# A Winograd-style 3x3 convolution: all input pairs as fp32 through one queue into nine fixed homes

## The chip, the cores and the metric

The kernel runs on one core of one Trainium2 chip. The metric is the device time in microseconds (us) of one execution; lower is better. Beside it stands a profile of one execution, whose span is the time from its first to its last instruction.

## The reference

A 3x3 convolution with padding 1, stride 1, over 16 images of 64 channels and 64 x 64 points, to 128 output channels, all in fp32:

```python
batch, c_in, h, w, c_out = 16, 64, 64, 64, 128
x_pad = np.pad(x, ((0, 0), (0, 0), (1, 1), (1, 1)), mode='constant')
for b in range(batch):
    for co in range(c_out):
        for ci in range(c_in):
            for kh in range(3):
                for kw in range(3):
                    output[b, co] += weight[co, ci, kh, kw] * x_pad[b, ci, kh:kh+h, kw:kw+w]
```

The input has 16.8 MB, the output 33.6 MB, the weights 0.3 MB.

## The kernel before

Two images make a pair: their 2 x 64 channels fill the 128 partitions, so a pair is one tile of 128 x 64 x 64 (16 KB per partition in fp32, 2 MB in all). There are eight pairs, p = 0 to 7.

Output rows are made two at a time. For rows 2j and 2j+1 the kernel makes three sums of products on TensorE: one over x[2j] + x[2j+1] with the middle weight row (group U), one for the even rows (group A, weight rows G21 and G0) and one for the odd rows (group Bt, G01 and G2). The output is A + U and Bt + U. The pair sums x[2j] + x[2j+1] are the tile `ss`, made by `sums` (line 76) on GpSimd, for pair 0 on VectorE. The fp16 input itself is the tile `xs`. A pair is cut into four blocks of 16 output rows. In each block TensorE runs U, A, Bt (line 150) into PSUM (8 banks, two for each group), ScalarE copies U to SBUF as `ut` (line 164), and VectorE adds it to A and Bt into the fp32 output tiles `ots` (lines 174 and 177), one tile for each of the two images.

Input comes in two ways. Pairs 0 to 3 are loaded in fp32 on SyncE's queue at the start (lines 45 and 49), as `x0` and `xf`, and ScalarE casts them to `xs` (line 101 for pair 0; line 169 for the others, four casts of 16 rows, two each in blocks 2 and 3 of the pair before). Pairs 4 to 7 are loaded by GpSimd's queue, and the transfer itself casts to fp16 (`load`, line 67): pair 4 before pair 0's work, pairs 5, 6, 7 after the sums issued in pairs 1, 2, 3.

Output goes out by `store` (line 106): the first image of a pair on SyncE's queue when its last block is added, the second image held back and issued on ScalarE's queue behind the first U copies of the next block (line 171). The last pair goes out in halves of 32 rows.

The tiles `x0`, `xf` and `ot` share one pool of eight places of 16 KB per partition (`opool`), taken in turn: pairs 0 to 3 take four places as input, the outputs of pairs 0 and 1 the other four, those of pairs 2 and 3 the input's places, those of pair 4 the places of pair 0's outputs, and so on. A place is written again only when its load's readers or its store are done. `xs` has five places of 8 KB, `ss` three, `ut` four. `keep` pins an instruction behind what was written before it on its own engine; the stores on SyncE and the loads on lines 42 to 49 are not pinned.

Of the kernel before, what the change touches and what calls it, by code (L numbers as in the profile page):

```python
# [8 lines left out]
F32 = mybir.dt.float32  # L9
F16 = mybir.dt.float16  # L10


@with_exitstack
def kernel(
    ctx: ExitStack,
    tc: tile.TileContext,
    x: bass.AP,
    weight: bass.AP,
    out: bass.AP,
):  # L20
    nc = tc.nc
    B, CI, H, W = x.shape
    CO = weight.shape[0]
    assert H == 64 and W == 64 and CI == 64 and CO == 128 and B % 2 == 0
    NP = B // 2
    RB = 8

    keep = tc.keep_in_program_order
    x_rows = x.rearrange("b c h w -> (b c) h w")
    out_rows = out.rearrange("b co h w -> b co h w")  # L30
    w_flat = weight.rearrange("co ci kh kw -> co (ci kh kw)")

    const = ctx.enter_context(tc.tile_pool(name="const", bufs=1))
    psum = ctx.enter_context(tc.tile_pool(name="psum", bufs=8, space=bass.MemoryType.PSUM))
    xpool = ctx.enter_context(tc.tile_pool(name="xpool", bufs=5))
    opool = ctx.enter_context(tc.tile_pool(name="opool", bufs=8))
    spool = ctx.enter_context(tc.tile_pool(name="spool", bufs=3))
    upool = ctx.enter_context(tc.tile_pool(name="upool", bufs=4))


    w_raw = const.tile([CO, CI * 9], F32)
    nc.sync.dma_start(w_raw, w_flat)
    x0 = opool.tile([128, H, W], F32, tag="ot", name="x0")
    cuts = [(0, 18), (18, 34), (34, 50), (50, 64)]
    nc.sync.dma_start(x0, x_rows[0:128, :, :])
    xf = {}
    for p in (1, 2, 3):
        xf[p] = opool.tile([128, H, W], F32, tag="ot", name="xf")
        nc.sync.dma_start(xf[p], x_rows[128 * p : 128 * p + 128, :, :])
    zeros = const.tile([128, 512], F16)  # L50
    keep(nc.vector.memset(zeros, 0.0))  # L51
    warm = psum.tile([128, 512], F32, tag="acc", name="warm")

    def spin(n):
        for _ in range(n):
            keep(nc.tensor.matmul(warm, zeros[:, 0:128], zeros))  # L56

    ident = const.tile([128, 128], F16)
    make_identity(nc, ident)
    w16 = const.tile([CO, CI * 9], F16)  # L60
    keep(nc.gpsimd.tensor_copy(w16, w_raw))  # L61

    xs = {p: xpool.tile([128, H, W], F16, tag="xs", name="xs") for p in range(4)}

    def load(p):
        xs[p] = xpool.tile([128, H, W], F16, tag="xs", name="xs")
        keep(nc.gpsimd.dma_start(xs[p], x_rows[128 * p : 128 * p + 128, :, :]))  # L67

    ss = {}

    def sums(eng, p, src, lo, n):
        if p not in ss:
            ss[p] = spool.tile([128, H // 2, W], F16, tag="ss", name="ss")
        v = src.rearrange("p (j i) c -> p j i c", i=2)
        keep(
            eng.tensor_add(  # L76
                ss[p][:, lo : lo + n, :], v[:, lo : lo + n, 0, :], v[:, lo : lo + n, 1, :]
            )
        )


    Wt = const.tile([128, 5, 3, CO], F16)
    G0, G21, G1, G01, G2 = range(5)

    def wrow(i):
        return Wt[:, i, :, :].rearrange("p t c -> p (t c)")

    for kh, g in ((1, G1), (2, G2), (0, G0)):
        wp = psum.tile([128, 512], F32, tag="acc", name="wp")
        for k in range(3):  # L90
            t = 3 * kh + k
            for q in (0, 64):
                keep(nc.tensor.matmul(wp[q : q + 64, k * CO : k * CO + CO], w16[:, t::9], ident))  # L93
        keep(nc.scalar.copy(wrow(g), wp[:, 0 : 3 * CO]))  # L94
    spin(10)
    keep(nc.gpsimd.tensor_sub(wrow(G21), wrow(G2), wrow(G1)))  # L96
    keep(nc.gpsimd.tensor_sub(wrow(G01), wrow(G0), wrow(G1)))  # L97
    load(4)
    for n, (lo, hi) in enumerate(cuts):
        sums(nc.vector, 0, x0, RB * n, RB)  # L100
        keep(nc.scalar.copy(xs[0][:, lo:hi, :], x0[:, lo:hi, :]))  # L101

    held = []

    def store(eng, p, b2, ot, lo, hi):
        return eng.dma_start(
            out_rows[2 * p + b2, :, lo:hi, :],
            ot.rearrange("p j i c -> p (j i) c")[:, lo:hi, :],
        )

    for p in range(NP):
        if p + 1 < NP:
            for lo in (0, 16):
                sums(nc.gpsimd, p + 1, xf.get(p + 1, xs[p + 1]), lo, 16)
        if p > 0 and p + 4 < NP:
            load(p + 4)
        ots = [
            opool.tile([128, H // 2, 2, W], F32, tag="ot", name="ot") for _ in range(2)
        ]
        for blk in range(4):  # L120
            j0 = blk * RB

            def group(wi_rows):

                tiles = [
                    psum.tile([128, RB, W], F32, tag="acc", name="acc") for _ in range(2)
                ]
                n = 3 * len(wi_rows)
                i = 0
                for wi, off in wi_rows:  # L130
                    for kw in (1, 0, 2):
                        c_lo, c_hi = max(0, 1 - kw), min(W, W + 1 - kw)
                        for b2 in range(2):
                            p0 = 64 * b2
                            lo, hi = j0, j0 + RB
                            if off is None:
                                rhs = ss[p][p0 : p0 + 64, lo:hi, c_lo + kw - 1 : c_hi + kw - 1]
                            else:
                                while 2 * lo + off < 0:
                                    lo += 1  # L140
                                while 2 * (hi - 1) + off > H - 1:
                                    hi -= 1
                                first = 2 * lo + off
                                last = 2 * (hi - 1) + off
                                rhs = xs[p][
                                    p0 : p0 + 64,
                                    first : last + 1 : 2,
                                    c_lo + kw - 1 : c_hi + kw - 1,
                                ]
                            nc.tensor.matmul(  # L150
                                tiles[b2][:, lo - j0 : hi - j0, c_lo:c_hi],
                                Wt[p0 : p0 + 64, wi, kw, :],
                                rhs,
                                start=i == 0,
                                stop=i == n - 1,
                            )
                        i += 1
                return tiles

            U = group([(G1, None)])  # L160
            us = []
            for b2 in range(2):
                ut = upool.tile([128, RB, W], F32, tag="ut", name="ut")
                keep(nc.scalar.copy(ut, U[b2]))  # L164
                us.append(ut)
            if p + 1 in xf:
                q = p + 1
                for lo in {2: (0, 16), 3: (32, 48)}.get(blk, ()):
                    keep(nc.scalar.copy(xs[q][:, lo : lo + 16, :], xf[q][:, lo : lo + 16, :]))  # L169
            while held:  # L170
                keep(store(nc.scalar, *held.pop(0)))
            A = group([(G21, 1), (G0, -1)])
            for b2 in range(2):
                nc.vector.tensor_add(ots[b2][:, j0 : j0 + RB, 0, :], A[b2], us[b2])  # L174
            Bt = group([(G01, 0), (G2, 2)])
            for b2 in range(2):
                nc.vector.tensor_add(ots[b2][:, j0 : j0 + RB, 1, :], Bt[b2], us[b2])  # L177
            parts = {3: (0, 64)} if p < NP - 1 else {1: (0, 32), 3: (32, 64)}
            if blk in parts:
                lo, hi = parts[blk]  # L180
                store(nc.sync, p, 0, ots[0], lo, hi)
                held.append((p, 1, ots[1], lo, hi))
    while held:
        keep(store(nc.scalar, *held.pop(0)))


# [28 lines left out]
```

## Time and profile before

| | |
|---|---|
| time, median of 3 runs (lowest to highest) | 126.33 us (126.21 to 126.34) |
| the profiled execution | 126.56 us |
| its span | 124.8 us |
| mean granted TensorE clock | 0.963 |
| first product of pair 0 (line 150) | 9.92 us |
| time from pair to pair (ScalarE's stores) | 12.81 us |

Times in a view are microseconds from the start of the span, unless marked ns. PE is TensorE (matmul), PEld its weight loads, DVE VectorE, ACT ScalarE, POOL GpSimd, SP SyncE; SPq, ACTq and POOLq are their instruction queues. A row with forty digits cuts the span into forty slices of 3.12 us and gives the busy share of each in tenths (9 is 90% or more); the DMA row is the mean over the core's 16 DMA engines, and the GB/s row is what they moved, where a casting transfer is counted by the bytes that it writes. A DMA queue's line has packets, MB, and the time that its packets took as a share of the time of 16 engines. A line of instructions has start, length, engine, source line, operation, output <- input, count, and in brackets the idle time before it and what ended that. A line of DMA issues has the count, KB of one transfer and the median time from issue to landing.

### The profile page before, as it was taken

How to read it: one execution, taken by the hardware profiler on the slowest of the kernel's cores; microseconds unless marked ns; L12 is line 12 of the kernel's file. 1: busy time of each engine (PE TensorE's matmuls, PEld its weight loads, DVE VectorE, ACT ScalarE, POOL GpSimd, SP SyncE). 2: the span in 40 equal slices, each digit the busy share in tenths (PEclk: the TensorE clock that was granted, in tenths of full speed). 3: DMA queues.
4: the chain of work that ended last, by engine and by line, in shares of the span. 5: the costliest groups of instructions: out<-in, count | busy, mean ns of one | idle time of the engine just before them, and what ended most of it. 6: DMA issues, size and time to landing. Idle time of an engine off the chain costs nothing.

```text
span 124.8 us, 2437 instructions
## 1 busy us (share of the span) xinstructions
PE 108.2 (87%) x988; PEld 49.3 (40%) x988; DVE 82.8 (66%) x133; ACT 52.0 (42%) x84; POOL 36.2 (29%) x27
## 2 busy tenths in 40 slices
PE   0699999999999999999999999999999999990000
PEld 0433444444444444444444444444444444440000
DVE  0016787878878787877777778777877787685000
ACT  4319749833993399333333333333333333330000
POOL 2360086294799202920067000940000000000000
PEclk9999999999999999999999999999999999999555
DMA  6899999999999999999999999999999999999991
GB/s 173 362 436 407 297 323 349 425 315 415 397 349 368 305 376 373 360 334 362 381 347 360 334 344 412 431 431 425 425 441 420 436 415 425 436 412 418 436 402 74
DMA packets 3898, 46.57 MB, mean 373 GB/s; under 512 B 432, under 2 KB 432, under 8 KB 560
## 3 DMA queue, kind: packets, MB, share of 16 engines
q1 hardware_dynamic: 2016, 25.46, 49.5%
q10 hardware_dynamic: 1296, 16.78, 31.6%
q0 software_dynamic: 576, 4.19, 16.1%
q8 instruction: 7, 0.11, 0.3%
q14 instruction: 3, 0.02, 0.0%
HBM read 17.07 MB, written 33.55 MB: 406 GB/s over the span
## 4 chain that ended last, share of the span: by engine, by line
PE 86%; DMA 2%; DVE 1%; issue 1%; POOL 1%; DVEq 0%
PE acc L150 81%; PE warm L56 4%; DMA w_raw<-in_weight_dram 2%; PE wp L93 1%; DVE ot L174 1%; POOL w L61 1%; DVE ot L177 0%; DVEq L210 0%; DVEq L174 0%
## 5 line engine op out<-in xcount | busy, mean ns | idle before, releaser
L150 PE MATMUL acc<-xs,Wt 64*128 64x504 f16 (+3 forms) x768 | 87.0, 373 | 0.0
L150 PEld LDWEIGHTS <-Wt 64*128 64x128 f16 x960 | 46.8, 94 | 56.2 <-issue 0.8
L164 ACT COPY ut<-acc 128x512 f32<-128x512 f32 x64 | 34.3, 588 | 52.9 <-issue 32.1
L174 DVE TENSOR_TENSOR ot<-acc,ut 128x512 f32<-128x512 f32 x64 | 41.2, 686 | 22.6 <-PE acc L150 18.3
L177 DVE TENSOR_TENSOR ot<-acc,ut 128x512 f32<-128x512 f32 x64 | 41.1, 684 | 0.0
L150 PE MATMUL acc<-ss,Wt 64*128 64x504 f16 (+1 forms) x192 | 26.0, 377 | 0.0
L76 POOL TENSOR_TENSOR ss<-xs 128x1024 f16<-128x1024 f16 x8 | 16.8, 2124 | 20.2 <-DMA xs<-in_x_dram 20.2
L76 POOL TENSOR_TENSOR ss<-xf 128x1024 f16<-128x1024 f32 x6 | 14.1, 2361 | 13.6 <-DMA xf<-in_x_dram 13.6
L169 ACT CAST xs<-xf 128x1024 f16<-128x1024 f32 x12 | 12.0, 1058 | 0.0
L76 DVE TENSOR_TENSOR ss<-x 128x512 f16<-128x512 f32 x4 | 2.5, 687 | 7.7 <-DMA x<-in_x_dram 7.7
L93 PE MATMUL wp<-ident,w 128*64 128x128 f16 x18 | 1.3, 328 | 4.3 <-POOL w L61 4.3
L101 ACT CAST xs<-x 128x1024 f16<-128x1024 f32 (+2 forms) x4 | 3.9, 1042 | 2.6 <-DMA x<-in_x_dram 2.6
L67 POOL DMA_DIRECT2D xs<-in_x_dram x4 | 2.4, 600 | 7.8 <-ACT xs L169 7.8
L56 PE MATMUL warm<-zeros 128*128 128x512 f16 x10 | 4.4, 631 | 0.0
L93 PEld LDWEIGHTS <-w 128*64 128x64 f16 x18 | 1.1, 210 | 4.3 <-POOL w L61 4.3
L94 ACT CAST Wt<-wp 128x384 f16<-128x384 f32 x3 | 1.2, 487 | 2.9 <-PE wp L93 2.9
L56 PEld LDWEIGHTS <-zeros 128*128 128x128 f16 x10 | 1.3, 143 | 2.3 <-issue 2.2
L94 ACT ACT_TABLE_LOAD x1 | 1.3, 1283 | 0.7 <-PEq L199 0.7
L96 POOL TENSOR_TENSOR Wt<-Wt 128x384 f16<-128x384 f16 x1 | 0.9, 907 | 1.7 <-ACT Wt L94 1.7
L61 POOL CAST w<-w_raw 128x576 f16<-128x576 f32 x1 | 0.7, 663 | 2.3 <-DMA w_raw<-in_weight_dram 2.3
L97 POOL TENSOR_TENSOR Wt<-Wt 128x384 f16<-128x384 f16 x1 | 0.9, 910 | 0.0
L51 DVE MEMSET zeros<- 128x256 uint32 x1 | 0.3, 272 | 0.9 <-PEq L199 0.9
(6 smaller groups left out, 0.9 us busy)
## 6 DMA issues: line engine op xcount, KB each, us to landing
out_dram<-ot SPq DMA_DIRECT2D x7, 2048.0 KB, 22.0
out_dram<-ot ACTq DMA_DIRECT2D x7, 2048.0 KB, 18.9
xf<-in_x_dram SPq DMA_DIRECT2D x3, 2048.0 KB, 22.1
xs<-in_x_dram POOLq DMA_DIRECT2D x4, 1024.0 KB, 23.4
x<-in_x_dram SPq DMA_DIRECT2D x1, 2048.0 KB, 7.6
out_dram<-ot SPq DMA_DIRECT2D x2, 1024.0 KB, 10.6
out_dram<-ot ACTq DMA_DIRECT2D x2, 1024.0 KB, 11.0
w_raw<-in_weight_dram SPq DMA_DIRECT2D x1, 288.0 KB, 2.8
```

What stands on the lines that cost most here:

```text
L56: keep(nc.tensor.matmul(warm, zeros[:, 0:128], zeros))
L61: keep(nc.gpsimd.tensor_copy(w16, w_raw))
L67: keep(nc.gpsimd.dma_start(xs[p], x_rows[128 * p : 128 * p + 128, :, :]))
L76: eng.tensor_add(ss[p][:, lo : lo + n, :], v[:, lo : lo + n, 0, :], v[:, lo : lo + n, 1, :])
L93: keep(nc.tensor.matmul(wp[q : q + 64, k * CO : k * CO + CO], w16[:, t::9], ident))
L94: keep(nc.scalar.copy(wrow(g), wp[:, 0 : 3 * CO]))
L101: keep(nc.scalar.copy(xs[0][:, lo:hi, :], x0[:, lo:hi, :]))
L150: nc.tensor.matmul(tiles[b2][:, lo - j0 : hi - j0, c_lo:c_hi], Wt[p0 : p0 + 64, wi, kw, :], rhs, start=i == 0, stop=i == n - 1,)
L164: keep(nc.scalar.copy(ut, U[b2]))
L169: keep(nc.scalar.copy(xs[q][:, lo : lo + 16, :], xf[q][:, lo : lo + 16, :]))
L174: nc.vector.tensor_add(ots[b2][:, j0 : j0 + RB, 0, :], A[b2], us[b2])
L177: nc.vector.tensor_add(ots[b2][:, j0 : j0 + RB, 1, :], Bt[b2], us[b2])
```

## The change

All eight pairs are loaded in fp32 on SyncE's queue, and ScalarE casts all of them (seven pairs on line 169's place). No load casts and GpSimd issues no DMA. The pool of eight places becomes nine homes with names, each of 16 KB per partition: E has two, T three, a, b, c and d one each.

- E first holds pairs 0 and 1 (one transfer each), then pairs 5 and 6 (one transfer, issued on SyncE behind pair 1's store), then the outputs of pair 7.
- T first holds pairs 2, 3 and 4 (one transfer of 6 MB, issued at the start behind pairs 0 and 1), then pair 7 in its first third (issued behind pair 3's store) and the outputs of pair 4 in the other two.
- a and b hold the outputs of pairs 0, 2 and 5; c and d those of pairs 1, 3 and 6.

Pair 6 is stored in halves, as pair 7 is. Pair 7's two images go out together, in one transfer for each half, on SyncE's queue; the other pairs still send one image on SyncE's queue and one on ScalarE's. SyncE's loads and stores are pinned in the order written. `xs` has three places instead of five.

```diff
-    xpool = ctx.enter_context(tc.tile_pool(name="xpool", bufs=5))
-    opool = ctx.enter_context(tc.tile_pool(name="opool", bufs=8))
+    xpool = ctx.enter_context(tc.tile_pool(name="xpool", bufs=3))
+    opool = ctx.enter_context(tc.tile_pool(name="opool", bufs=1))
...
+    def room(home, n):
+        return opool.tile([128, n, H, W], F32, tag=home, name=home)
...
-    x0 = opool.tile([128, H, W], F32, tag="ot", name="x0")
-    nc.sync.dma_start(x0, x_rows[0:128, :, :])
     xf = {}
-    for p in (1, 2, 3):
-        xf[p] = opool.tile([128, H, W], F32, tag="ot", name="xf")
-        nc.sync.dma_start(xf[p], x_rows[128 * p : 128 * p + 128, :, :])
+    def load(t, k, *ps):
+        n = len(ps)
+        src = x_rows[128 * ps[0] : 128 * ps[-1] + 128, :, :]
+        keep(
+            nc.sync.dma_start(t[:, k : k + n, :, :], src.rearrange("(t q) h w -> q t h w", q=128))
+        )
+        for i, p in enumerate(ps):
+            xf[p] = t[:, k + i, :, :]
+
+    E = room("E", 2)
+    T = room("T", 3)
+    load(E, 0, 0)
+    load(E, 1, 1)
+    load(T, 0, 2, 3, 4)
+    x0 = xf[0]
...
-    xs = {p: xpool.tile([128, H, W], F16, tag="xs", name="xs") for p in range(4)}
-
-    def load(p):
-        xs[p] = xpool.tile([128, H, W], F16, tag="xs", name="xs")
-        keep(nc.gpsimd.dma_start(xs[p], x_rows[128 * p : 128 * p + 128, :, :]))
-
+    xs = {0: xpool.tile([128, H, W], F16, tag="xs", name="xs")}
...
-    load(4)
...
-    def store(eng, p, b2, ot, lo, hi):
-        return eng.dma_start(
-            out_rows[2 * p + b2, :, lo:hi, :],
-            ot.rearrange("p j i c -> p (j i) c")[:, lo:hi, :],
+    def store(eng, b, t, lo, hi):
+        n = t.shape[1]
+        keep(
+            eng.dma_start(
+                out_rows[b : b + n, :, lo:hi, :].rearrange("b c h w -> c b h w"),
+                t[:, :, lo:hi, :],
+            )
         )
 
     for p in range(NP):
         if p + 1 < NP:
+            xs[p + 1] = xpool.tile([128, H, W], F16, tag="xs", name="xs")
             for lo in (0, 16):
-                sums(nc.gpsimd, p + 1, xf.get(p + 1, xs[p + 1]), lo, 16)
-        if p > 0 and p + 4 < NP:
-            load(p + 4)
+                sums(nc.gpsimd, p + 1, xf[p + 1], lo, 16)
+        if p == 4:
+            images = [T[:, 1:2, :, :], T[:, 2:3, :, :]]
+        elif p == NP - 1:
+            images = [room("E", 2)]
+        else:
+            images = [room(h, 1) for h in ("ab" if p in (0, 2, 5) else "cd")]
         ots = [
-            opool.tile([128, H // 2, 2, W], F32, tag="ot", name="ot") for _ in range(2)
+            t[:, k, :, :].rearrange("p (j i) c -> p j i c", i=2)
+            for t in images
+            for k in range(t.shape[1])
         ]
...
-            if p + 1 in xf:
+            if p + 1 < NP:
                 q = p + 1
                 for lo in {2: (0, 16), 3: (32, 48)}.get(blk, ()):
                     keep(nc.scalar.copy(xs[q][:, lo : lo + 16, :], xf[q][:, lo : lo + 16, :]))
             while held:
-                keep(store(nc.scalar, *held.pop(0)))
+                store(nc.scalar, *held.pop(0))
...
-            parts = {3: (0, 64)} if p < NP - 1 else {1: (0, 32), 3: (32, 64)}
+            parts = {3: (0, 64)} if p < NP - 2 else {1: (0, 32), 3: (32, 64)}
             if blk in parts:
                 lo, hi = parts[blk]
-                store(nc.sync, p, 0, ots[0], lo, hi)
-                held.append((p, 1, ots[1], lo, hi))
-    while held:
-        keep(store(nc.scalar, *held.pop(0)))
+                store(nc.sync, 2 * p, images[0], lo, hi)
+                if len(images) > 1:
+                    held.append((2 * p + 1, images[1], lo, hi))
+                if p == 1:
+                    load(room("E", 2), 0, 5, 6)
+                if p == 3:
+                    T = room("T", 3)
+                    load(T, 0, 7)
```

## The prediction

> **What bounds the kernel now.** I read the page first: engine shares, then the 40 slices, then the queues.
>
> ```profile
> span 124.8 us, 2437 instructions
> PE 108.2 (87%) x988; PEld 49.3 (40%) x988; DVE 82.8 (66%) x133; ACT 52.0 (42%) x84; POOL 36.2 (29%) x27
> PE   0699999999999999999999999999999999990000
> DMA  6899999999999999999999999999999999999991
> GB/s 173 362 436 407 297 323 349 425 315 415 397 349 368 305 376 373 360 334 362 381 347 360 334 344 412 431 431 425 425 441 420 436 415 425 436 412 418 436 402 74
> q1 hardware_dynamic: 2016, 25.46, 49.5%
> q10 hardware_dynamic: 1296, 16.78, 31.6%
> q0 software_dynamic: 576, 4.19, 16.1%
> HBM read 17.07 MB, written 33.55 MB: 406 GB/s over the span
> ```
>
> TensorE looks like the bound at 87%, but its row ends four slices early while the DMA row is full from slice 3 to slice 39. The three transfer queues (q1 is SyncE's, q10 ScalarE's, q0 the casting loads) add up to 97.2% of all DMA time. The chain of waits (start, length, work) and the DMA issues of the last stretch say the same.
>
> ```profile
> 9.99 101.39 PE acc L150 x948
> 113.32 0.60 DVE ot L177
> out_dram<-ot ACTq DMA_DIRECT2D x1, 1024.0 KB, 9.9
> ```
>
> The last addition ends at 113.92, the last store is issued at 113.95 and lands 9.9 us later, at 123.85. Its 2.1 MB (it and its sister on SyncE) need only 5.0 us at 420 GB/s, so they wait in a queue first: the DMA reaches them at about 118.2. Had they been issued 3.3 us later (118.2 less 113.95 and about 1 us from issue to first byte), nothing would have changed. So the end is: DMA start, plus DMA work, plus every moment in which the DMA has nothing to do. Compute has 3.3 us of slack.
>
> To price a packet I asked for the DMA queues in four windows: 9 to 22 us (fp32 and casting loads together), 22 to 24 (fp32 loads alone), 78 to 100 (16-KB stores), 110 to 120 (mostly 8-KB stores). Columns: packets, MB, share of 16 engines.
>
> ```profile
> q1 hardware_dynamic: 226, 3.44, 62.6%
> q0 software_dynamic: 143, 1.05, 38.6%
> q1 hardware_dynamic: 69, 0.87, 101.6%
> q10 hardware_dynamic: 319, 4.70, 50.2%
> q10 hardware_dynamic: 255, 2.22, 52.4%
> ```
>
> An fp32 load packet (16,384 bytes) costs 1.016 x 2 us x 16 engines / 53 = 0.612 us; a casting packet (reads 16 KB, writes 8) 0.386 x 13 x 16 / 128 = 0.627; a store packet 0.502 x 22 x 16 / 287 = 0.616; two 8-KB store packets 2 x 0.309 = 0.619. All kinds cost nearly alike: about 429 GB/s counted by the larger side.
>
> **The change, part by part.** Terms are sums against the profiled execution (126.56 us, its span 124.8 and 1.76 around it); it lies 0.23 above the median of 126.33, to which I apply the difference.
>
> *Four casting loads become fp32 loads.* HBM bytes stay at 17.07 and 33.55 MB; of those read 8.39 MB change their kind, 32 packets per engine: 32 x (0.612 - 0.627) = -0.5 us of DMA work. That would be the whole gain of removing the cast, since writing half the bytes saved no time. Bounds from the same rows: 0 if an fp32 load mixed with others costs 0.626 x 13 x 16 / 210 = 0.620 and store turns eat the rest, -0.5 at best. I take -0.4.
>
> *Pair 6 in halves.* 4.19 MB, 16 packets of 16 KB per engine become 32 of 8 KB: 16 x (0.619 - 0.616) = +0.05 us, at most +0.1. Earlier issue gains nothing while the DMA is full.
>
> *ScalarE casts.* Sixteen more at 1.058 us, 17 us in all, two each in blocks 2 and 3 of pairs 3 to 6. In pairs 0 to 2 these casts exist already and the pair still takes 12.81 us, as in later pairs (ScalarE's stores at 24.30, 37.11, 49.92, 62.73, 75.53). Zero; the cover is ScalarE's 2.1 us of idle before each copy. GpSimd's sums read fp32: 8 x (2.36 - 2.12) = 1.9 us more, and four issues of 0.6 us leave it; it idles 71%. Zero.
>
> *Loads of pairs 0, 1 and 2-4 at once.* Pair 0 is first in the queue as before: compute starts as before. Until about 28.5 us the DMA has 40 load packets per engine either way (32 fp32 and 8 casting; now 40 fp32), so pairs 2 to 4 land where pair 3 landed, 2.6 + 29.1 = 31.7 at the latest. Pair 2 is wanted by ScalarE's cast at 30.99 and GpSimd's sums, first half needed when TensorE enters pair 2 at 35.54: 31.7 + 2.36 = 34.1. The cover is 1.4 us.
>
> *Nine homes instead of a pool of eight.* Homes a and b (pair 0) are written again by pair 2, c and d by pair 3; before, pair 0's places came back in pair 4. Here is the nearest point, ScalarE's store of pair 1 and VectorE's first addition of pair 2:
>
> ```profile
> 37.11 0.34 ACTq L106 DMA_DIRECT2D out_dram<-ot  x1
> 37.68 1.29 DVE L174 TENSOR_TENSOR ot<-acc,ut 128x512 f32<-128x512 f32 x2 [0.60 <-PE acc L150]
> ```
>
> When are a and b free? Until then the DMA owes 0.29 + 10.49 (five pairs) + 4.19 = 14.97 MB. Before, it had moved by 37.44 us (12 slices) 13.25 MB, plus 1.36 hidden because casting loads count half: 14.6. The rest takes 0.9 us: 38.3, and landing adds under 0.9 (last packets start after 123.0, landing 123.85). So VectorE waits from 37.68 to about 39: 1.3 us. TensorE's eight PSUM banks carry one block and a third, so perhaps 0.5 us reaches it, inside the 3.3. Homes c and d are issued at 36.5 and 37.1, share the DMA alone, 16 packets x 0.612 = 9.8 us: 48.1, landed by 49; wanted at 37.68 + 12.81 = 50.5. Behind that, c's store on SyncE has the 4-MB load of pairs 5 and 6 behind it, and behind that pair 2's store: the load lands at about 63, wanted by casts at 30.99 + 3 x 12.81 = 69. Pair 7 lands by 82, wanted by its casts at 95. Zero for all of these.
>
> *Does the DMA run dry?* This is the term that would cost. The opening work ends at 38.3; pair 1's first store is issued at 36.5, and a first byte came 1.0 us after issue at the start (0.74 to 1.72): 37.5. No gap, with 0.8 us to spare; 0 to +0.3 for engines that finish early. I take +0.1. Afterwards 8.4 MB (pair 1 and pairs 5, 6) cover 38 to 58, and each pair's 9.8 us of stores plus pair 7's load keep a backlog to the end.
>
> *The last pair in one transfer on SyncE.* Issued at 113.95, when its second image is ready; before, SyncE's half went at 113.32. Under a full DMA, zero. That one queue alone can fill the DMA is the 101.6% row.
>
> *One hiccup stays.* Between 26 and 28 us the windows show 279 and 213 GB/s, with no casting load; about 1.1 us are lost just after the first stores are issued (23.7, 24.3). I know no cause and keep it; without it the sum is 1.1 lower, less about 0.4 because the dry spot at 37 then opens.
>
> Sum: -0.4 + 0.05 + 0.1 = about -0.3: **126.0 us**. About 0.2%, 0.25 us, is what this measurement can tell from no change, so the forecast stands just beyond it.
>
> **Rivals.** (1) *Homes too late, slower.* If SyncE's load of pairs 5 and 6 (16 packets) got all its turns ahead of ScalarE's store d, that store would run after c and the load: 38.3 + 24 x 0.612 = 53.0, +4.9, landed 58.6 instead of 49, wanted at 51.1. VectorE loses 7.5, TensorE some 6.5, less the 3.3 of slack: +3.2, **129.5**. It decides once d lands after about 55; half that lateness costs nothing. For it: ScalarE's first store, issued 24.30, moved no byte until 28.9 beside SyncE's load. Against: from 29 on q1 and q10 take turns evenly (61% and 42% in one microsecond). 14%.
>
> (2) *The DMA runs dry, slower.* If pair 1's stores need those 4.6 us to start, bytes come at 41.1, not 38.3: +2.5 with the gain deducted, **128.8** at worst, 127.5 if half of it. The 4.6 us can be the packets already taken in by busy engines, which leave no gap; the idle start took 1.0. 14%.
>
> (3) *The engines' lag goes, faster.* At the end the windows give 303 GB/s at 121, 123 at 122: some engines finish 1.1 us behind the rest. If the casting queue made that lag it disappears: **124.9**. Against: each engine gets the same 32 casting packets, and the last of them landed at 78. 9%. The Trainium skill, DMA: Bandwidth & Descriptors, Latency and other measured facts, says that two of the engines are usually slower and guesses at the software queue's descriptor rings as cause; no view here separates engines.
>
> (4) *Fewer, larger transfers gain by themselves.* Pair 0 took 7.6 us where 4.9 are bytes; three transfers fewer at 2.7 would give 8 us, **118**. The 22 to 24 window holds the end of one load and the start of the next at 434 GB/s, so nothing is lost between them. 2%. The Trainium skill, DMA: Bandwidth & Descriptors, Anatomy of one DMA, fits 2.0 us plus bytes at 436 GB/s to one DMA; as an estimate, three fewer in a row would save 6 us by it, and the trace does not agree for queued ones.
>
> (5) *The last pair's halves share one tile.* If the write of rows 32 to 63 waited for the store of rows 0 to 31 of both images, additions would start at 117 and the end come near **131**. The rows are disjoint. 4%.
>
> **How the numbers follow.** Forecast 51% (own range 125.6 to 126.5; three fifths of it beyond the bound of faster, a third within it), hiccup gone 6% (125.3), rivals as above. Faster: 0.31 + 0.06 + 0.09 + 0.02 = 0.48, cut to 0.45 for small TensorE delays at several homes; same 0.17; slower 0.38. The range 124.9 to 128.4 leaves out (4), (5), the worst of (1) and (2), two in ten.
>
> **What would show it.** Right: no casting queue, DMA row without a hole at slices 12 and 13, VectorE's L174 waiting about 1 us for a store near 38, last landing 0.3 us earlier, TensorE's pair still 12.81. Wrong: a DMA slice of 7 or less near 38 (rival 2), VectorE waiting for a store for several us near 51 (rival 1), TensorE's row reaching slices 37 to 39, or waits for a load by ScalarE's casts.

## The result, and the profile after

The changed kernel takes 127.88 us (median of 4 runs, 127.74 to 128.02) beside 126.34 us (126.21 to 126.43) for the kernel before on the same chip: a ratio of 1.0123, 95% interval 1.0105 to 1.0141. It is 1.5 us slower, where 0.3 us faster was forecast. The profiled execution took 127.77 us with a span of 126.0 us; before it was 126.56 and 124.8. So the span grew by 1.2 us.

The page of the changed kernel, with the rows that the prediction read before:

```profile
span 126.0 us, 2446 instructions
PE   0589999999999999999999999999999999990000
DMA  5999999999999999999999999999999999999970
GB/s 149 386 432 437 432 427 416 437 323 427 458 411 421 421 414 434 427 375 427 458 427 416 427 416 453 437 421 421 416 427 453 432 388 434 424 419 424 437 320 18
q1 hardware_dynamic: 2944, 35.95, 68.4%
q10 hardware_dynamic: 1152, 14.68, 27.5%
HBM read 17.07 MB, written 33.55 MB: 402 GB/s over the span
```

TensorE's row still ends in slice 35 (counted from 0), and the DMA row has no hole. The casting queue is gone. The GB/s row dips twice, each time where a load runs just after stores have been issued: slice 8 (323, before 315) and slice 17 (375, new). The queues' packets take 95.9% of 126.0 us, that is 120.8 us for each DMA engine; before it was 97.2% of 124.8, 121.3 us. There is less transfer work, by 0.5 us, and a later end.

The chain of waits (start, length, work) and the DMA issues of the last stretch:

```profile
41.35 70.49 PE acc L168 x638
...
113.23 0.60 DVE E L195
113.83 0.60 DVEq L232
```

```profile
out_dram<-E SPq DMA_DIRECT2D x2, 2048.0 KB, 11.5
```

The last addition ends at 113.83, against 113.92 before, and the last store is issued at 114.45, 0.5 us later than before. That costs nothing, as the store ahead of it in the queue lands at 118.0 on the median engine. So compute doesn't make the end later. What does is seen in the DMA queues from 118 to 126 us, in forty slices of 0.2 us. Before:

```profile
DMA  9999999999999997963726310000000000000000
GB/s 410 451 451 410 451 451 410 451 451 410 451 451 410 410 492 328 410 287 164 328 123 287 164 41 0 41 0 0 0 0 0 0 0 0 0 0 0 0 0 0
```

After:

```profile
DMA  9899799699599699557446321100000000000000
GB/s 532 369 410 532 328 410 573 287 451 573 246 451 532 287 451 573 246 246 328 205 205 287 164 82 41 82 0 41 0 41 41 0 41 0 0 0 0 0 0 0
q1 hardware_dynamic: 240, 1.81, 53.5%
```

One 8-KB packet that starts in a slice makes 41 GB/s. Before, the last one starts at 123.0 us. After, single packets go on to 124.4, and the last two landings are at 123.67 and 125.16: one of the 16 engines is alone at work for about 1.5 us. The trace has the 16 landings of each transfer, one from each engine. For the last transfer:

| last transfer's 16 landings, us | first | median | mean | last | last less mean |
|---|---|---|---|---|---|
| before | 121.57 | 122.86 | 122.56 | 123.82 | 1.26 |
| after | 121.76 | 122.92 | 122.71 | 125.16 | 2.45 |

The mean engine ends 0.15 us later, the slowest 1.34 us later. So in the profiled execution 1.2 of the 1.34 us are **spread**, the last engine's distance from the mean one. This is one execution of each kernel.

### The profile page after: what moved, and what is told of

The parts are those of the page before. It is cut to its first block, busy times and chain, and to the rows that moved or that the text cites. A ratio compares the mean times of both kernels' runs of the same rounds, so it can differ in the third digit from the quotient of the medians.

```text
span 126.0 us, 2446 instructions
## 1 busy us (share of the span) xinstructions
PE 108.0 (86%) x988; PEld 56.6 (45%) x988; DVE 82.4 (65%) x133; ACT 66.8 (53%) x100; POOL 35.8 (28%) x23
## 4 chain that ended last, share of the span: by engine, by line
PE 81%; DMA 6%; DVE 2%; issue 1%; DVEq 0%; SPq 0%
PE acc L168 81%; DMA E<-in_x_dram 6%; DVE E L192 1%; DVE ss L85 1%; DVE b L192 1%; DVE E L195 0%; DVEq L232 0%; SPq L45 0%; DVEq L192 0%
## 5 line engine op out<-in xcount | busy, mean ns | idle before, releaser
L168 PEld LDWEIGHTS <-Wt 64*128 64x128 f16 x960 | 54.4, 94 | 49.8 <-issue 2.2
L85 POOL TENSOR_TENSOR ss<-T 128x1024 f16<-128x1024 f32 x8 | 18.6, 2367 | 28.5 <-DMA T<-in_x_dram 28.5
L85 POOL TENSOR_TENSOR ss<-E 128x1024 f16<-128x1024 f32 x6 | 14.0, 2364 | 25.4 <-DMA E<-in_x_dram 25.4
L187 ACT CAST xs<-T 128x1024 f16<-128x1024 f32 x16 | 16.0, 1056 | 1.0 <-DMA T<-in_x_dram 1.0
L192 DVE TENSOR_TENSOR a<-acc,ut 128x512 f32<-128x512 f32 x12 | 8.3, 689 | 9.4 <-ACT ut L182 5.6
L192 DVE TENSOR_TENSOR c<-acc,ut 128x512 f32<-128x512 f32 x12 | 8.3, 691 | 7.6 <-PE acc L168 5.7
L187 ACT CAST xs<-E 128x1024 f16<-128x1024 f32 x12 | 12.0, 1058 | 0.0
L192 DVE TENSOR_TENSOR d<-acc,ut 128x512 f32<-128x512 f32 x12 | 8.2, 681 | 0.8 <-PE acc L168 0.8
L195 DVE TENSOR_TENSOR c<-acc,ut 128x512 f32<-128x512 f32 x12 | 8.3, 688 | 0.0
L195 DVE TENSOR_TENSOR a<-acc,ut 128x512 f32<-128x512 f32 x12 | 8.2, 684 | 0.0
L192 DVE TENSOR_TENSOR b<-acc,ut 128x512 f32<-128x512 f32 x12 | 8.2, 680 | 0.0
L195 DVE TENSOR_TENSOR d<-acc,ut 128x512 f32<-128x512 f32 x12 | 8.2, 680 | 0.0
L195 DVE TENSOR_TENSOR b<-acc,ut 128x512 f32<-128x512 f32 x12 | 8.2, 680 | 0.0
L192 DVE TENSOR_TENSOR E<-acc,ut 128x512 f32<-128x512 f32 x8 | 5.2, 686 | 2.8 <-PE acc L168 2.8
L195 DVE TENSOR_TENSOR E<-acc,ut 128x512 f32<-128x512 f32 x8 | 5.1, 684 | 0.0
```

Of the source, the lines that this page charges most:

```text
L85: eng.tensor_add(ss[p][:, lo : lo + n, :], v[:, lo : lo + n, 0, :], v[:, lo : lo + n, 1, :])
L168: nc.tensor.matmul(tiles[b2][:, lo - j0 : hi - j0, c_lo:c_hi], Wt[p0 : p0 + 64, wi, kw, :], rhs, start=i == 0, stop=i == n - 1,)
```

## Experiments

The first theory was that something in the changed order of transfers at the tail, in the halves, or in the merged loads makes one engine late; the rival was that fp32 loads in the middle of the run cost more than their packets' usual time. Later runs took the queues apart. Ratios are against runs of the kernel before on the same chip (its medians 126.47 to 126.66). "Mean" and "last" are landings of the last transfer, as in the table above.

**x1_tail: the last pair's images on SyncE and ScalarE again.**

```diff
-            images = [room("E", 2)]
+            E = room("E", 2)
+            images = [E[:, 0:1, :, :], E[:, 1:2, :, :]]
...
+    while held:
+        store(nc.scalar, *held.pop(0))
```

> The changed kernel, but pair 7's two images go out as before: one on SyncE's queue, one held back for ScalarE's. Theory A (the last transfers stand on one queue alone, so the slowest of the 16 DMA engines ends later): 126.4 us, 1.2 to 1.5 below the changed kernel's 127.88, the last landing about 1 us after the median engine's. Theory B (the slowest engine's lag comes from the loads having become fp32 on SyncE's queue) and theory C (from the merged transfers) expect no change: 127.7 to 128.0.

128.52 us, ratio 1.014 (1.0089 to 1.0191). The loss stays. The tail's queue is not its cause.

**x2_whole6: pair 6 stored whole.**

```diff
-            parts = {3: (0, 64)} if p < NP - 2 else {1: (0, 32), 3: (32, 64)}
+            parts = {3: (0, 64)} if p < NP - 1 else {1: (0, 32), 3: (32, 64)}
```

> The changed kernel, but pair 6 is stored whole (16-KB packets) instead of in halves. If the doubled number of packets feeds the slowest engine's lag: 0.3 to 1 us below 127.88. Theories A, B and C: 127.8, at most 0.1 us saved by fewer packets.

128.41 us, 1.0115 (1.0064 to 1.0166). The halves are not the whole cause; the interval leaves room for a part of some tenths of a us.

**x3_split: each pair in a transfer of its own.**

```diff
-    load(T, 0, 2, 3, 4)
+    load(T, 0, 2)
+    load(T, 1, 3)
+    load(T, 2, 4)
...
-                    load(room("E", 2), 0, 5, 6)
+                    E = room("E", 2)
+                    load(E, 0, 5)
+                    load(E, 1, 6)
```

> The changed kernel, but pairs 2, 3, 4 and pairs 5, 6 come by one transfer each instead of one of three and one of two. Theory C (merged transfers cause the second stretch of slow load packets at 52 to 54 us, 0.34 us a engine, and the lag): 126.8 to 127.4, no slow load packets near 53 us. Theories A and B: 127.8 to 127.9.

128.35 us, 1.013 (1.0082 to 1.0178). Not the merging either: the slow load packets came again, at 53 to 56 us.

In the profiled executions of x2_whole6 and x3_split the mean is 123.29 and 123.46 and the last 125.19 and 125.29. Against the changed kernel's 122.71 and 125.16 the mean engine is later there and the spread smaller (1.9 and 1.8 us). So how the loss divides into mean and spread is not the same in every run. (x1_tail's profiled execution, 129.50 us, is the slowest of its six and isn't compared here.)

**y1_tailsp: the kernel before, with only the last pair's second image moved to SyncE.**

```diff
-                held.append((p, 1, ots[1], lo, hi))
+                if p < NP - 1:
+                    held.append((p, 1, ots[1], lo, hi))
+                else:
+                    store(nc.sync, p, 1, ots[1], lo, hi)
```

> The kernel before, with both images of the last pair on SyncE's queue, as separate transfers. Theory A: slower by about 1 us, 127.3. Theories B and C: 126.3 to 126.5, as before.

126.71 us, 0.9991 (0.9965 to 1.0017): no difference, mean 122.40, last 123.82. Together with x1_tail this clears the one queue at the end, which the prediction had at zero.

**z1_cast56: pairs 5 and 6 as casting loads on GpSimd again** (in the changed kernel, with four places for `xs`).

```diff
...
+        if p in (1, 2):
+            q = p + 4
+            xs[q] = xpool.tile([128, H, W], F16, tag="xs", name="xs")
+            keep(nc.gpsimd.dma_start(xs[q], x_rows[128 * q : 128 * q + 128, :, :]))
...
-                if p == 1:
-                    load(room("E", 2), 0, 5, 6)
```

> The changed kernel, but pairs 5 and 6 come as casting loads on GpSimd's queue, as before (four places for xs); pair 7, T and the nine homes stay. Theory B (an fp32 load on SyncE's queue in mid-run, beside stores, brings slow packets at its start and when the next stores are issued, and these feed the slowest engine's lag): ratio to the kernel before 1.000 to 1.004, no slow packets at 44 and 52 us. Theory D (the homes, the order of the stores or the extra casts cost it): ratio stays at 1.011 to 1.014.

129.01 us, 1.0171 (1.0117 to 1.0226). It doesn't tell the theories apart, because the homes became late. The waits of this kernel (waited for; us in all, times, longest):

```profile
DVE c L197 <- DMA out_dram<-c: 4.9, 1, 4.9
```

Home c's store had landed by 47.44 us on the median engine and at 55.9 on the last two. VectorE's first addition into c came at 56.06, and compute ended 3.3 us later than in the changed kernel. VectorE waits for a home, as in rival 1, but because of two engines and not of the queue as a whole.

**z3_actload: the load of pairs 5 and 6 on ScalarE's queue.**

```diff
...
+            if p == 2 and blk == 0:
+                load(room("E", 2), 0, 5, 6, eng=nc.scalar)
...
-                if p == 1:
-                    load(room("E", 2), 0, 5, 6)
```

> The changed kernel, but the one transfer of pairs 5 and 6 is issued on ScalarE's queue behind pair 1's second store. If it matters that the load stands on SyncE's queue ahead of pair 2's first store: ratio 1.004 or less. If any fp32 load in mid-run does it, whichever queue: 1.011 to 1.014, with slow packets at the load's start and some 3 us after the next stores are issued.

128.05 us, 1.0101 (1.0069 to 1.0133). Mean 122.92, last 125.21. The slow load packets described below came at 52.2 to 55.1 us again, now in ScalarE's queue. The loss stays, whether SyncE's or ScalarE's queue holds the load; both also hold stores.

**w1_fp32_5: the kernel before, with pair 5 alone in fp32 on SyncE's queue.** Halves, tail and the other casting loads are as before. The load takes a place of the pool of eight, so the outputs behind it move on by one place.

```diff
-        if p > 0 and p + 4 < NP:
+        if p > 1 and p + 4 < NP:
...
+                if p == 1:
+                    xs[5] = xpool.tile([128, H, W], F16, tag="xs", name="xs")
+                    xf[5] = opool.tile([128, H, W], F32, tag="ot", name="xf")
+                    keep(nc.sync.dma_start(xf[5], x_rows[640:768, :, :]))
```

> The kernel before, but pair 5 comes in fp32 on SyncE's queue behind pair 1's first store and ScalarE casts it; pairs 4, 6 and 7 stay casting loads. Theory B: slower by about half of the change's loss, ratio 1.004 to 1.008, with slow packets beside that load that the kernel before doesn't have. Theory D: 0.998 to 1.001.

127.79 us, 1.0096 (1.0059 to 1.0133). This one edit gives most of the loss, but not as spread alone. The last landing, of SyncE's transfer, moved from 123.82 (ScalarE's) to 125.02, by 1.20 us. The mean of SyncE's last transfer moved from 121.60 to 122.62 and that of ScalarE's, the last one issued, from 122.56 to 123.24: the mean engine is later too, by about 0.7 us. The packets took longer, 122.25 us in all for the mean engine beside 121.75. VectorE also waits 2.0 us for a place of the pool, which it never did before; compute's end didn't move (last store issued at 114.21).

**w2_pool5: the same single fp32 load, on GpSimd's queue.**

```diff
-        if p > 0 and p + 4 < NP:
+        if p > 1 and p + 4 < NP:
...
+        if p == 1:
+            xs[5] = xpool.tile([128, H, W], F16, tag="xs", name="xs")
+            xf[5] = opool.tile([128, H, W], F32, tag="ot", name="xf")
+            keep(nc.gpsimd.dma_start(xf[5], x_rows[640:768, :, :]))
```

> The kernel before, but pair 5 comes in fp32, without a cast, on GpSimd's queue at the place where its casting load stood; ScalarE casts it. The same with SyncE's queue cost 0.96%. Theory B1 (the queue matters: a load on the hardware queues beside stores): 0.998 to 1.003. Theory B2 (the fp32 bytes written to SBUF, twice those of the casting load, or the home that they take from the output, matter whatever the queue): 1.007 to 1.013.

132.97 us, 1.0477 (1.0436 to 1.0517). Inconclusive, because in this order a place of the pool came free late.

```profile
DVE ot L178 <- DMA out_dram<-ot: 8.4, 1, 8.4
```

VectorE waits 8.4 us, and the DMA then runs short in several slices. What the load costs by itself can't be read from it.

**m1_sp, m2_cast, m3_pool: the transfers alone.** The convolution is left out: pairs 0 to 3 are loaded on SyncE, then a tile of zeros is stored 16 times, alternately on SyncE and ScalarE, with the loads of pairs 4 to 7 between the stores. The three differ only in those loads; the lines marked by a name are that run's.

```diff
     for p in range(8):
         keep(nc.sync.dma_start(out_rows[2 * p, :, :, :], src))
         keep(nc.scalar.dma_start(out_rows[2 * p + 1, :, :, :], src))
         if p in (1, 2, 3, 4):
-            fp32(nc.sync, p + 3)      # m1_sp
+            cast(p + 3)               # m2_cast: casting, on GpSimd
+            fp32(nc.gpsimd, p + 3)    # m3_pool
```

> Transfers alone, no convolution: the weights, pairs 0 to 3 in fp32 on SyncE's queue, then 16 stores of a zero tile (SyncE and ScalarE in turn) with pairs 4 to 7 in fp32 on SyncE's queue among them. 192 packets of 16 KB for each DMA engine at 0.611 us and the weights: about 119 us of span from the first packet. If the loss lies in the DMA itself, this is 0.7 to 1.5 us longer than m2_cast with its last engine late; if it needs the compute engines beside it, the two differ by less than 0.5 us and the casting one is the longer, by 32 x 0.013 = 0.4.

> As m1_sp, but pairs 4 to 7 come as casting loads on GpSimd's queue. See m1_sp: shorter than it by 0.7 to 1.5 us if the loss lies in the DMA itself, else longer by about 0.4.

> As m1_sp, but pairs 4 to 7 come in fp32 on GpSimd's queue, without a cast. Theory B1: as m2_cast. Theory B2: as m1_sp.

**m4_split: the same transfers with all loads on SyncE and all stores on ScalarE** (the edit is against m1_sp).

```diff
-    for p in range(4):
-        fp32(nc.sync, p)
     for p in range(8):
-        keep(nc.sync.dma_start(out_rows[2 * p, :, :, :], src))
-        keep(nc.scalar.dma_start(out_rows[2 * p + 1, :, :, :], src))
-        if p in (1, 2, 3, 4):
-            fp32(nc.sync, p + 3)
+        fp32(nc.sync, p)
+    for p in range(16):
+        keep(nc.scalar.dma_start(out_rows[p, :, :, :], src))
```

> Transfers alone: the weights and all eight pairs in fp32 on SyncE's queue, all 16 stores on ScalarE's queue, so that no queue holds both kinds. m1_sp, with both kinds on SyncE's queue, took 127.16 us, m3_pool, with the mid loads on GpSimd's, 124.32. If the loss needs loads and stores in one queue: 124.2 to 124.9. If it needs only fp32 loads on a hardware queue beside stores on the other: 126 or more.

| transfers alone | median, us (lowest to highest) | mean | last | last less mean |
|---|---|---|---|---|
| m1_sp: mid loads fp32 on SyncE, between stores | 127.16 (126.75 to 128.3) | 122.06 | 124.21 | 2.16 |
| m2_cast: mid loads casting, GpSimd | 124.83 (124.62 to 124.94) | 121.73 | 122.10 | 0.37 |
| m3_pool: mid loads fp32, GpSimd | 124.32 (124.26 to 124.64) | 121.37 | 121.54 | 0.17 |
| m4_split: loads SyncE, stores ScalarE | 124.16 (124.04 to 124.32) | 121.27 | 121.52 | 0.25 |

Two things are shown here. Dropping the cast is worth 0.5 us of time (m2_cast less m3_pool), about as forecast. And the same bytes cost 2.8 to 3.0 us more when the fp32 loads stand in a queue between stores, with no compute near. The DMA queues of m1_sp from 118 to 126 us:

```profile
DMA  9959959779979972211111111110000000000000
GB/s 573 410 246 655 410 246 655 328 328 492 492 328 492 492 328 82 82 82 82 82 82 82 82 82 82 82 82 0 0 0 0 0 0 0 0 0 0 0 0 0
q1 hardware_dynamic: 110, 1.49, 43.6%
```

From slice 15 on (121.0 us) there are 82 GB/s for 2.4 us, one 16-KB packet started in each slice of 0.2 us. As a packet takes 0.611 us, these are three engines: thirteen are done. Their landings say the same (123.90, 124.04 and 124.21, all others by 121.82). m3_pool, from 118 to 123 us in slices of 0.125 us, stops at once:

```profile
DMA  9609990099900999009990000000000000000000
q1 hardware_dynamic: 86, 1.15, 53.6%
```

In m1_sp the three fall behind during the load of 92.6 to 97.3 us (median landings): in the store ahead of it the last engine is 0.7 us behind the median one, in this load three are 2.2 to 2.6 behind, and three single load packets of 1.8 to 1.9 us instead of 0.611 lie in between. From there the lag stays, 2.57 us in the last transfer. It need not stay: in the kernel before, SyncE's store that lands at 71 us has its last engine 3.8 us behind the median, the run's last transfer 1.0.

**v1_poolmid: the changed kernel with pairs 5, 6 and 7 as single fp32 loads on GpSimd's queue,** as m3_pool would suggest; **v2_poolall** also has pairs 2 to 4 there.

```diff
...
+        if p == 3:
+            E = room("E", 2)
+            load(E, 0, 5, eng=nc.gpsimd)
+            load(E, 1, 6, eng=nc.gpsimd)
+        if p == 4:
+            T = room("T", 3)
+            load(T, 0, 7, eng=nc.gpsimd)
...
-                if p == 1:
-                    load(room("E", 2), 0, 5, 6)
-                if p == 3:
-                    T = room("T", 3)
-                    load(T, 0, 7)
```

> The changed kernel, but pairs 5, 6 and 7 come in fp32 on GpSimd's queue, one transfer each, issued late enough to leave homes c and d their turns (5 and 6 behind the sums for pair 4, 7 behind those for pair 5). Theory B1 (fp32 loads in mid-run cost time only on a hardware queue): ratio to the kernel before 0.994 to 1.001, no slow load packets at 52 us, the slowest DMA engine less than 1.3 us behind the median. Rival (stores and loads mixed cost it whatever the queue, or the homes do): 1.010 or more.

> As v1_poolmid, and pairs 2, 3 and 4 come on GpSimd's queue too, one transfer each, issued behind the weight sums. Theory B1: the slow packets at 26 us go as well (0.72 us a engine): ratio 0.988 to 0.996. If those at 26 us come from the first stores themselves: as v1_poolmid.

128.65 us, 1.0167 (1.0126 to 1.0208), and 128.76 us, 1.0157 (1.0117 to 1.0198). The cure of the transfers alone doesn't work in the kernel. Means are 123.83 and 123.37, last landings 125.71 and 125.62: here the mean moves too. v1_poolmid's page shows where, in slices 15 to 17 (47.5 to 57 us):

```profile
GB/s 166 378 424 450 414 419 445 440 321 424 414 434 440 429 427 341 375 357 440 424 440 414 434 419 424 434 419 440 419 429 440 419 414 414 427 429 422 429 378 23
```

GpSimd's loads have three quarters of the DMA's time then, and their packets take 761 ns on average in place of 611.

**n1_split, n2_before, n3_one5: all stores on ScalarE's queue,** in the changed kernel, in the kernel before, and in w1_fp32_5 (shown: n2_before).

```diff
-                store(nc.sync, p, 0, ots[0], lo, hi)
+                held.append((p, 0, ots[0], lo, hi))
                 held.append((p, 1, ots[1], lo, hi))
```

> The changed kernel with all its loads on SyncE's queue as before, but all its stores on ScalarE's queue. If loads and stores in one queue are the cause of the loss (as with the transfers alone: 127.2 with shared queues, 124.2 without), 1.004 of the kernel before or less, no fp32 load packets of 0.7 us or more after 40 us, and the last engine within 0.7 us of the median one. If the cause lies in fp32 loads that run alone while stores are issued, or in the homes, 1.010 or more again.

> The kernel before with all its stores on ScalarE's queue, as a control for the run beside it: 0.998 to 1.002 if that queue alone is as good as the two (its fp32 loads end before its stores begin, so no queue holds both at once either way). Below 0.997 if two store queues cost something by themselves.

> The kernel before with pair 5 loaded in fp32 on SyncE's queue, and all stores on ScalarE's. With the stores on both queues this load cost a ratio of 1.0096. If sharing the queue is the cause, 1.002 or less; if the fp32 load in the middle of the run is the cause wherever the stores are, 1.007 or more.

n1_split took 135.64 us, 1.0715 (1.0681 to 1.075), and is inconclusive. The store of home b now stands behind that of home a in one queue. And the load of pairs 5 and 6, with no store ahead of it on SyncE's queue any more, goes out at 23.2 us instead of 36.8 and takes turns with them. So b's store lands on its last engine at 49.0, in the changed kernel at 40.1:

```profile
DVE b L192 <- DMA out_dram<-b: 8.9, 1, 8.9
```

```profile
PE   0699999999991009999999999999999999999200
DMA  5999999999999999924995699999999999999693
```

VectorE stands still for 8.9 us, TensorE has a hole in slices 12 to 14, and the DMA runs short in 17, 18, 21 and 22. That is rivals 1 and 2 in one picture, 8 us slower than the changed kernel.

n2_before took 127.29 us, 1.0075 (1.0043 to 1.0107), n3_one5 127.80 us, 1.0088 (1.006 to 1.0115). Their means are 122.55 and 122.58, the kernel before's being 122.56; their last landings are 124.47 and 124.67. So moving the stores alone already makes the last landing 0.65 us later, all of it spread. Loads and stores in one queue, the reading of m1_sp, is therefore not needed for a spread: no queue of n2_before ever holds both, and from 32 us on it has no fp32 load. n3_one5 adds at most a few tenths of a us (the intervals overlap), but it doesn't answer its question: with no store ahead of it, pair 5's load went out at 13.1 us and had landed by 41.9, where w1_fp32_5 issued it at 36.9. It is no load in the middle of the run. In both profiled executions a packet of the instruction queue (see o1_third) of 1.2 to 1.5 us also starts at 127.2 to 127.4 us, behind the last landing, and 2.8 and 3.0 us lie outside the span instead of 1.8; that part of their profiled times is no spread.

**o1_third: late instruction fetches away.** Seven times in a run, about every 13 us, the trace of the changed kernel has one packet of some 0.9 us in a queue that it calls instruction (q8), and right behind it one load or store packet of about 1.0 us. Perhaps the last one, at 101.2 us, makes the late engine.

```diff
+                kws = (1, 0, 2) if p < 4 else (1,)
...
-                    for kw in (1, 0, 2):
+                    for kw in kws:
```

> The changed kernel with only one of the three kernel columns multiplied in pairs 4 to 7 (the other two thirds of these pairs' products are left out), so that TensorE has 320 matmuls fewer and the instruction fetches after about 75 us go away, two of seven; loads, stores and homes are as in the changed kernel and the transfers stay the bound. If the fetch at 101 us, which stretches one engine's packets by about 1.2 us, makes the slowest engine end 2.2 us behind the median, it ends 1.2 us or less behind, and the ratio is 1.004 or less. If the slow fp32 load packets of 27, 45 and 53 us fell unevenly on the engines, the slowest still ends 2 us behind and the ratio is 1.010 or more.

132.19 us (130.23 to 132.9), 1.0346 (1.029 to 1.0402). Other things moved with the edit: VectorE waits 7.1 us for home a's stores, and the granted clock is 0.846, so no exact size is read from it. But two fetches are gone, the last of the other five comes at 90.1 us, and the spread is larger than ever. DMA queues from 123 to 126 us:

```profile
DMA  2502070207002200020002000200020002000200
q1 hardware_dynamic: 26, 0.16, 12.4%
```

One engine alone sends its packets, one behind the other, to the end of the window and beyond (last landing 129.85, mean 123.39). The lag is older than the last fetch: home c's store lands at 79.1 on the median engine and at 89.1 on the last. A fetch at 101 us isn't needed for a late engine.

No version beat both kernels. y1_tailsp is level with the kernel before.

## Why the prediction was wrong, step by step

**What bounds the kernel:** right. Compute ended where it had ended, and a later end came from the DMA alone. One reading in it is off: 123.85 less 5.0 us is 118.9, not 118.2, so that the slack is 3.9 instead of 3.3 us, which changes nothing here.

**The cast's price:** right as packet time, and worth nothing in the kernel. The queues' time fell from 121.3 to 120.8 us, as the terms -0.4 and +0.05 say, and m2_cast against m3_pool shows 0.5 us in the transfers alone. Yet the mean engine ended 0.15 us later. Casting packets overlap others in time: in the prediction's window from 9 to 22 us the two queues' shares add up to 101.2%, and in the changed kernel the single queue has 99.9% there. Such shares count a packet where it starts, and the prediction's own window with fp32 loads alone has 101.6%, so the two windows by themselves prove little. The records of the whole run do: stretches with more than 16 packets at work add up to 1.48 us for each engine before, and to 0.91 after.

```profile
q1 hardware_dynamic: 355, 5.55, 99.9%
```

A packet's duration was taken for the time it occupies an engine. From the trace's records of all queues, packet time plus what lies outside it was 121.75 + 0.82 us for the mean engine before, and 121.29 + 1.42 after: the lost overlap costs 0.6 us (1.48 less 0.91), more than the 0.46 gained.

**Halves, casts on ScalarE, sums on GpSimd, one queue at the tail:** zero or nearly so, as far as the runs tell (x1_tail, x2_whole6 within its interval, y1_tailsp; from pair 2 on pairs still follow each other at 12.81 us).

**The homes:** the mechanism was right, with waits longer than worked out. The changed kernel's timeline shows when ScalarE issues home d's store, and VectorE's first additions into a (pair 2) and d (pair 3):

```profile
36.91 0.35 ACTq L116 DMA_DIRECT2D out_dram<-d  x1
...
40.01 0.69 DVE L192 TENSOR_TENSOR a<-acc,ut 128x512 f32<-128x512 f32 x1 [3.13 <-ACT ut L182]
...
52.45 0.69 DVE L192 TENSOR_TENSOR d<-acc,ut 128x512 f32<-128x512 f32 x1 [0.77 <-PE acc L168]
```

VectorE starts pair 2 at 40.01, where 39 was expected and 37.68 was the time before. The bracket names ScalarE, which was long done (37.72); what came last was the stores of a and b, landing at 39.89 and 40.08. Home d's store landed at 52.33 on its last engine, not by 49. Loads came at 65.3 (63 expected) and 89.6 (82). The slack took all of it.

**The DMA runs dry:** it did not, as forecast. That the measured 127.88 us lies inside the stated range is luck: the range reached that far for the two slower rivals, and neither a dry DMA near 38 us nor a long wait for home d near 51 is in the trace.

**"One hiccup stays":** it stayed (load packets of up to 1.39 us at 26 to 28 us), but not alone. A second one came where the next fp32 load ran just after stores had been issued. DMA queues of the changed kernel from 52 to 55 us:

```profile
q1 hardware_dynamic: 56, 0.92, 81.4%
q10 hardware_dynamic: 15, 0.25, 19.1%
```

A packet of q1 takes 0.814 x 3 us x 16 / 56 = 698 ns, not 612. Before, in the same window, SyncE's store packets take 0.377 x 3 x 16 / 29 = 624 ns:

```profile
q1 hardware_dynamic: 29, 0.48, 37.7%
q10 hardware_dynamic: 25, 0.41, 31.8%
q0 software_dynamic: 24, 0.20, 31.2%
```

Summed over the run, though, time above the usual durations is the same in both profiles (33.6 and 32.9 us over 16 engines). In this execution the slow packets don't make the mean engine late; in w1_fp32_5 and x3_split, where packets took 0.5 and 0.7 us more in all for each engine (122.25 beside 121.75, 121.97 beside 121.29), they do. That fp32 loads are what slows the packets isn't shown: z1_cast56 has store packets of 1.2 us at 45 us, with no fp32 load under way.

**The step that failed** is the form of the sum: "DMA start, plus DMA work, plus every moment in which the DMA has nothing to do". That holds for the mean engine, and there it missed by 0.45 us (-0.3 forecast, +0.15 measured), which is the lost overlap, a cost that the price of the cast had left out. The end is set by the slowest of 16 engines, and in the profiled execution the spread grew by 1.2 us (1.26 to 2.45), a term the sum didn't have. Only rival 3 spoke of it, and only as a lag that could go away. It took the casting queue for a possible cause of the lag; without that queue it doubled. The Trainium skill, DMA: Bandwidth & Descriptors, Latency and other measured facts, guesses at the software queue's descriptor rings as what slows two of the engines. The trace of the changed kernel doesn't support this as the cause here: it has no packet in that queue and the larger lag, and m3_pool, which uses it, has a spread of 0.17 us.

**What stays open:** why an engine falls behind. A late engine is not new in the changed kernel: in the load that ends at 29 us the last one is 2.7 us behind the median before and 3.0 after, yet at the end 1.0 and 2.2. Shown: an fp32 load in the middle of the kernel before makes its end later, by mean and spread together (w1_fp32_5); all stores in one queue, without such a load, bring spread alone (n2_before); with the transfers alone, fp32 loads between stores in one queue bring it, and two ways of separating them don't (m1_sp against m3_pool and m4_split). Long single packets lie where the lag begins in m1_sp. What makes those packets long, and why the lag gathers on one to three engines, no run here shows; nor why one run loses more by the mean and another more by the spread. The two kernels' other differences (order of stores, homes) may also have a part that wasn't separated: no run changed the homes alone. That instruction fetches add to the lag isn't excluded, only that one at 101 us is needed.

## What to carry to other kernels

Where transfers set the end, ask when the slowest DMA engine ends and not only how much work there is: compare the last transfer's 16 landings (of each queue, where two end together), or look for a long low tail in the last slices of the GB/s row. An advantage of a few tenths of a us from cheaper packets is smaller than what another arrangement of queues does to the spread (0.2 to 2.2 us in the transfers alone, 1.3 and 2.5 in the two kernels), so such a change should be forecast with that spread as its range. And a stretch that runs slow for no known reason is a term of the next estimate: find what runs in it, and ask whether the change brings more of that.

## What the hardware showed beyond expectation

- The same 50.6 MB on the same 16 engines took from 124.16 to 127.16 us by the choice of queues and order alone (m4_split, m1_sp). The Trainium skill, DMA: Bandwidth & Descriptors, Issuing engines are not separate DMA queues, says that transfers interleave on the same engines whoever issues them, and that issuing from several engines saves only the time of issue. The packets' usual durations agree (611 ns in either queue), the 3.0 us don't.
- A casting load's packet lasts longer than an fp32 one (624 against 611 ns) but overlaps its neighbours, so that in the kernel it cost no more; halving the written bytes saved nothing (m2_cast 124.83 us, m3_pool 124.32).
- fp32 load packets slowed to 698 ns on average (52 to 55 us), and singly to 1.9 us in m1_sp.
- One engine's late packets can hold a whole home: in z1_cast56 the last two engines brought c's store 8.4 and 8.5 us after the median one, and VectorE waited 4.9 us for them.
